# An encoder trunk on one core: when sums of weight blocks are formed by DMA, and in which order ACT and DVE split them

## The chip, the cores and the metric

The kernel runs on one core of a Trainium2 chip. The metric is the device time in microseconds of one execution, the median of several runs. TensorE multiplies matrices (its instructions are PE in the profile, its weight loads PEld), VectorE (DVE) and ScalarE (ACT) work element by element, GpSimd (POOL) and SyncE (SP) here mostly issue DMAs. Each engine works through its own queue in order, and the engines wait for each other through semaphores.

## The reference, cut to what matters

One layer of an encoder on x of 512 tokens by 1024 channels, all in float32:

```
x = x + token_mixer(rmsnorm(x))                      # HGRN2 and mLSTM scans
x = x + cross_attention(rmsnorm(x), rmsnorm(mem))    # 4 heads, 256 memory tokens
x = x + square(relu(rmsnorm(x) @ w_up)) @ w_down     # w_up 1024 x 4096, w_down 4096 x 1024
return rmsnorm(x)
```

The change touches the last product of the cross-attention (`@ w_o`), the weights streamed ahead of it, and above all the third line, the MLP.

## The kernel before

**Float32 out of three products.** Every matrix is split into a high half that TensorE's fp32r takes exactly and a low half that is the rest: ACT writes `hi = copy(src)`, DVE writes `lo = src - hi` (`split_out`, both at L348). A product is hi*hi + hi*lo + lo*hi, three matmuls (L351 to L353, in the MLP L1603 to L1605 and L1314 to L1316). So each weight block costs ACT one copy of 128x1024 and DVE one subtraction of 128x1024 (`wh` and `wl` in the profile) before TensorE can use it. Three buffers each hold the loaded blocks (`st`), the high halves (`wh`) and the low halves (`wl`).

**Seven products in place of eight.** The last product of the cross-attention and the two of the MLP use a scheme of Strassen's kind: a two by two block product in seven block products P1 to P7. Some multiply plain weight blocks (P1, P2, P3), the others sums of weight blocks (P5, P7, P6, P4), and the activation side too enters in sums ("forms"). P7 and P4 build on one chain of sums, P6 on it as well.

**Stages.** The MLP goes through the hidden width in four quarters. Each quarter has an "up" stage (even number `st`: 0, 2, 4, 6; function `up`) and a "down" stage (odd: 1, 3, 5, 7; function `by_blocks`). A stage has 14 jobs: P1 to P7, each for two halves g = 0 and 1 (a and b). A job of an up stage is 24 matmuls of 256 columns, one of a down stage 12 matmuls of 512 columns. The order of the jobs is written out by hand in `MORDER` (L1221): stage 0 has 1a 1b 2a 2b 5a 5b 6a 6b 7a 7b 4a 3a 4b 3b, stages 2, 4 and 6 have 1a 5a 1b 6a 2a 3a 7a 5b 6b 4a 2b 7b 3b 4b, stages 1, 3 and 5 have P1 P5 P6 P2 P7 P3 P4 with a before b, and stage 7 has P1 P5 P2 P6 P3 P7 P4. TensorE's order is this order; on the other engines a scheduler orders the instructions, by their place in the program, a priority (`tc.high_priority`) and added dependencies. `behind(a, b)` adds a dependency without a semaphore: it fixes the order where both stand on one engine. `after(a, b)` adds one with a semaphore.

**Where the sums of weights come from.** Three ways:

- *Form steps.* `make_forms` (L309) forms the sums of the up stages (P5, P7, P6, P4), of stage 1 (P5, P7, P6) and of stages 3, 5 and 7 (P7) in DRAM (`form_P`): a plain load or a copy of another form, issued on SP, then an accumulating DMA issued on POOL. 88 steps in all. They are doled out by a budget: `weights` (L283) is called once for each streamed weight block ahead of the cross-attention's last product, and calls `allow(n)` (L250), which issues steps until the budget is used up; a step on SP costs 1 and one on POOL costs 2. A step on SP is put behind the last weight load, one on POOL waits for the last split on DVE. What is left over is issued in the MLP by `mahead` (L1283), 2 units in every second job.
- *Sums of the down stages.* P5, P6 and P4 of stages 3, 5 and 7 (and P6 and P4 of stage 1) are formed in SBUF, in `msum` (tile `as`): `sum_base` (L1243) loads the first term on SP, `sum_add` (L1253) adds the second on POOL. They are due at a job number: `msplit(n)` (L1257), which splits the weights of job n, first issues what is due by n. P4's sum follows P6's in the same buffer.
- *Loads.* All other blocks are loaded into `st` by `mload`. `mahead(n)` calls `msplit` for jobs n to n+2 and `mload` for n+3 to n+6.

**The activation side.** For stage 0, `norm_half` (L1462) makes the forms of the normalized input; the seventh form P7 is split at L1491, P4 and P3 after it. In an up stage the products leave PSUM through ACT and DVE, and small functions form and split the inputs of the down stage: `first` (difference for P5, L1564), `by_p5` (square for P2, L1568), `second` (P6, L1574), `by_p3` (P3, L1578), `by_p7` (P7, L1582), each for a half g. Those that are not needed at once are called from inside the down stage: `turn` (L1656) lists before which job of the down stage each is put.

Of the kernel before, what the change touches and what calls it, by code (L numbers as in the profile page):

```python
# [80 lines left out]
def trunk(ctx: ExitStack, tc: tile.TileContext, x, mem, wpk, vec, cst, lmask, rmask, rows, out):  # L81
# [60 lines left out]
    def behind(a, b):  # L142

        tc.add_manual_dep(a.ins, b.ins.name, mybir.DependencyInfo(mybir.DependencyClass.NoSync, mybir.DependencyReason.DATA),
                          reason="order of an engine")
# [73 lines left out]
    turn = [0]  # L219
# [30 lines left out]
    def allow(n):  # L250

        budget[0] += n
        while budget[0] > 0:
            o = next(form_steps, None)
            if o is None:
                return
            budget[0] -= 1 if o.ins.engine == mybir.EngineType.SP else 2
            if o.ins.engine == mybir.EngineType.SP:
                behind(o, last_load[0])
            else:  # L260
                after(o, last_made[0])
                accs.append(o)
# [20 lines left out]
    def weights(key):  # L283
        i = SIDX[key]
        with (tc.high_priority() if i > 2 else ExitStack()):
            for n in range(i, i + 3):
                split(n)
            load(i + 3)
        allow(0 if i < 6 else 1 if key[1] == "kv" else 2.5 if i < 45 else 2)
        return hl_tiles[i]  # L290

    mforms = {}
# [959 lines left out]

    def sum_add(st, p, g):  # L1253
        o = mfill(gp, msum[p != "P5"][:, g * 1024:g * 1024 + 1024], st, g, (1, 0) if p == "P4" else (0, 0), True)
        behind(o, last_made[0])

    def msplit(n):  # L1257
        if n >= len(MJ):
            return
        if n not in mhl:  # L1260
            for w in [w for w in due if w[0] <= n]:
                due.remove(w)
                w[1](*w[2:])
            st, p, g = MJ[n]
            mload(n)
            hi, lo = T("wh", 1024, 3, F32R), T("wl", 1024, 3, F32R)
            made = split_out(hi, lo, mst[n])
            last_made[0] = made[1]
            if st % 2 and (p, g) == ("P5", 0):
                for a, b in zip(made, early["P5", 1]):  # L1270
                    behind(a, b)
            if n == 1:
                q_made[0] = made
            mhl[n] = (hi, lo)
            if st % 2 and p == "P6":
                due.append((n + 1, sum_add, st, "P4", g))
            if st % 2 and p in ("P5", "P4") and st < 7:
                q = {"P5": "P5", "P4": "P6"}[p]
                due.append((n + 3, sum_base, st + 2, q, g))
                due.append((n + 7, sum_add, st + 2, q, g))  # L1280
        return mhl[n]

    def mahead(n):  # L1283
        with tc.high_priority():
            for m in range(n, n + 3):
                msplit(m)
            for m in range(n + 3, n + 7):
                mload(m)
        if n % 2:
            allow(2)  # L1290
        return mhl[n]

# [169 lines left out]
    def norm_half(u):  # L1462

        ps = smb()
        for t in range(2):
            pe.transpose(ps[:, t * P:t * P + P], rt[u][:, t:t + 1].to_broadcast([P, P]), ident)
        with tc.high_priority():
            row = sc.activation(rrow[:, u * 256:u * 256 + 256], ps[:, 0:256], AF.Copy)
            if u == 1:
                behind(row, x_made[0][0])  # L1470
            for p, x in ((("P1", fx[0, 0]), ("P2", fx[0, 1])) if u == 0 else (("P5", sraw[0]),)):
                for h in range(2):
                    t_ = times_r(x, u, h)
                    if (p, h) in (("P2", 0), ("P5", 0)):
                        behind(t_, x_made[0][1])
                    made = part_split(p, x, h)
                    if p != "P5" and h == 1:
                        x_made[0] = made
                    if (p, h) == ("P1", 1):
                        for a, b in zip(q_made[0], made):  # L1480
                            behind(a, b)
        if u == 0:
            return
        d = sraw[0]
        x1, x3_, x2_, x4 = fx[0, 0], fx[0, 1], fx[1, 0], fx[1, 1]
        v.tensor_tensor(out=d, in0=d, in1=x1, op=ALU.subtract)
        split_out(*xf["P6"], d)
        for h in range(2):
            times_r(x4, 1, h)
        v.scalar_tensor_tensor(out=x1, in0=d, scalar=-1.0, in1=x4, op0=ALU.mult, op1=ALU.subtract)  # L1490
        p7 = split_out(*xf["P7"], x1)  # L1491
        p4 = split_out(*xf["P4"], x4)
        x3_made = v.tensor_tensor(out=x3_, in0=x3_, in1=d, op=ALU.add)
        for a in (x3_made, p4[1]):
            behind(a, p7[1])
        split_out(*xf["P3"], x3_)
# [53 lines left out]
    def up(st):  # L1550
# [2 lines left out]
        fl = dict(skip_group_check=True)  # L1553

        def square(t, src):
            sc.activation(t, src, AF.Relu)
            sc.activation(t, t, AF.Square)

        def form(p, g, src, buf):
            t = buf(F32R)  # L1560
# [1 line left out]
            forms[p, g] = t  # L1562

        def first(g):  # L1564
            v.tensor_tensor(out=y[3, g], in0=y[2, g], in1=y[3, g], op=ALU.subtract)
            form("P5", g, y[3, g], A4)

        def by_p5(g):  # L1568
            z = y[1, g]
            v.tensor_tensor(out=z, in0=C[g], in1=z, op=ALU.subtract)  # L1570
            square(z, z)
            form("P2", g, z, G4)

        def second(g):  # L1574
# [12 lines left out]
        for n, (p, g) in enumerate(MORDER[st]):  # L1587
            hi, lo = mahead(len(JOBS) * st + n)
            if p == "P1":
                A[g] = smb()  # L1590
            if p == "P2":
                B[g] = mmb()
            if p == "P5":
                C[g] = mmb()
            ps = B[g] if p == "P2" else C[g] if p in ("P5", "P3") else A[g]
            xh, xl = xf[p]
            for k in range(2):
                o = ps[:, k * 256:k * 256 + 256]
                for kt in range(4):
                    z = slice(k * 512 + kt * P, k * 512 + kt * P + P)  # L1600
                    m = slice(kt * 256, kt * 256 + 256)
                    new = k == kt == 0 and p in ("P1", "P2", "P5")
                    pe.matmul(o, lhsT=hi[:, z], rhs=xh[:, m], start=new, stop=False, **fl)  # L1603
                    pe.matmul(o, lhsT=hi[:, z], rhs=xl[:, m], start=False, stop=False, **fl)  # L1604
                    pe.matmul(o, lhsT=lo[:, z], rhs=xh[:, m], start=False, stop=kt == 3, **fl)  # L1605
                after_product()
            if p == "P1":
                y[0, g] = msum[g][:, 2048:2560]
                with tc.high_priority():
                    sc.activation(y[0, g], ps, AF.Copy)  # L1610
            elif p == "P2":
                with tc.high_priority():
                    v.tensor_tensor(out=y[0, g], in0=y[0, g], in1=ps, op=ALU.add)
                square(y[0, g], y[0, g])
                form("P1", g, y[0, g], yt)
            elif p == "P5":
                y[3, g] = T2()[:, 0:512]
                with tc.high_priority():
                    sc.activation(y[3, g], ps, AF.Copy)
            elif p == "P6":  # L1620
                y[1, g] = rrow[:, (1 - g) * 512:(1 - g) * 512 + 512]
                with tc.high_priority():
                    sc.activation(y[1, g], ps, AF.Copy)
            if p in ("P3", "P6") and {("P3", g), ("P6", g)} <= set(MORDER[st][:n + 1]) and (st == 0 or g == 0):
                by_p5(g)
            if p == "P7":
                with tc.high_priority():
                    v.tensor_tensor(out=y[3, g], in0=y[3, g], in1=ps, op=ALU.subtract)
                square(y[3, g], y[3, g])
                form("P4", g, y[3, g], A4)  # L1630
            elif p == "P4":
                y[2, g] = T2()[:, 0:512]
                with tc.high_priority():
                    square(y[2, g], ps)
                    first(g)
                if g == 0:
                    second(g)
                    by_p7(g)
                elif st:
                    by_p5(g)  # L1640
        sta = [{} for _ in range(4)]
# [11 lines left out]
                        fn(h)  # L1653
                    hand(h)

        turn = ((("P1", 1), second, 1), (("P5", 1), by_p3, 0), (("P6", 0), by_p7, 1), (("P2", 0), by_p3, 1))  # L1656
        if st == 6:
            turn = ((("P1", 1), second, 1), (("P5", 1), by_p3, 0), (("P2", 0), by_p3, 1), (("P6", 0), by_p7, 1))
        hand(0)
        hand(1)  # L1660
        return sta, ready
# [97 lines left out]
```

## Time and profile before

| | us |
|---|---|
| median of 3 runs | 827.46 |
| lowest and highest of them | 826.39, 829.32 |
| the profiled execution, its time | 825.79 |
| the profiled execution, its span | 824.0 |
| PE busy in it | 803.1 |
| DVE, ACT, POOL busy | 618.6, 486.1, 95.4 |

The span runs from the first to the last instruction; the rest of the profiled execution's time lies around it. TensorE's clock was granted in full (0.998 of the span). In the views, a line such as L348 can be that of a helper, so that groups are told apart by their tiles: `wl<-st,wh` is the low half of a streamed weight block, `yT<-a` the high half of an activation form. Matmuls overlap, so that one lasts longer than the distance to the next. `SPq` rows are DMA issues, and a DMA's landing is the end of its transfer.

The stages in this execution: the cross-attention's last product ends and stage 0 begins at about 493 us, stage 1 at 539, stage 2 at 579, stage 3 at 619, stage 4 at 657, stage 5 at 697.5, stage 6 at 736.4, stage 7 at 776.7; the last matmul ends at 815.4.

### The profile page before, as it was taken

The page shows a single profiled execution, that of the slowest core. Times are in us where ns is not written, and L with a number is a line of the kernel's source. Part 1 is how long each engine was busy: PE and PEld are TensorE (multiplying, and loading weights), DVE is VectorE, ACT ScalarE, POOL GpSimd, SP SyncE. Part 2 cuts the span into 40 slices and gives each one's busy share as a digit, 9 for nine tenths or more (in the row PEclk, how much of TensorE's full clock was granted, in tenths as well). Part 3 has the DMA queues.
Part 4 walks back from the last instruction along what each step waited for, and adds up shares of the span by engine and source line. Part 5 has one row for each costly group of instructions (what it writes and reads, how often), then busy time and mean ns, then how long its engine had stood idle before and what let it go on. Part 6 is the DMA issues. An engine that isn't in the chain of part 4 may idle for free.

```text
span 824.0 us, 14080 instructions
## 1 busy us (share of the span) xinstructions
PE 803.1 (97%) x5438; PEld 693.2 (84%) x5438; DVE 618.6 (75%) x1033; ACT 486.1 (59%) x854; POOL 95.4 (12%) x130
## 2 busy tenths in 40 slices
PE   8999999999999999999999999899999999999995
PEld 6788788886888989887888889887998899789984
DVE  6568975699469988555567979897489658875995
ACT  5247464445578475455545678773586458546854
POOL 2000111220230011221111003010001000100001
PEclk9999999999999999999999999999999999999999
DMA  7368889588688676887884357768866696668552
GB/s 278 118 238 257 216 181 280 174 197 254 159 230 252 198 221 203 237 193 218 203 224 108 85 122 212 248 163 247 267 199 158 218 282 198 180 200 266 179 153 103
DMA packets 56597, 167.26 MB, mean 203 GB/s; under 512 B 5393, under 2 KB 5521, under 8 KB 56530
## 3 DMA queue, kind: packets, MB, share of 16 engines
q1 hardware_dynamic: 41200, 126.04, 43.7%
q0 software_dynamic: 15040, 39.85, 26.8%
q8 instruction: 43, 0.70, 0.3%
q10 hardware_dynamic: 290, 0.47, 0.2%
q14 instruction: 24, 0.20, 0.1%
HBM read 164.24 MB, written 48.23 MB: 258 GB/s over the span
## 4 chain that ended last, share of the span: by engine, by line
PE 72%; DVE 11%; DMA 6%; issue 5%; ACT 5%; POOL 1%; POOLq 0%; ACTq 0%; DVEq 0%
PE mm L351 11%; PE mm L352 11%; PE mm L353 11%; PE sm L1315 5%; PE sm L1316 4%; PE sm L1314 4%; DVE wl L348 4%; PE sm L1604 2%; DMA st<-in_wpk 2%; PE sm L1605 2%; PE sm L1603 2%; ACT wh L348 2%; DMA st<-form_P 2%; PE mm L1604 1%; PE mm L1605 1%
## 5 line engine op out<-in xcount | busy, mean ns | idle before, releaser
L348 DVE TENSOR_TENSOR wl<-st,wh 128x1024 fp32r<-128x1024 f32 x165 | 201.5, 1224 | 104.0 <-ACT wh L348 103.1
L348 ACT ACTIVATE wh<-st 128x1024 fp32r<-128x1024 f32 x165 | 174.2, 1058 | 171.2 <-PE mm L352 44.0
L351 PE MATMUL mm<-xT,wh 128*128 128x512 f32 x288 | 115.5, 402 | 0.0
L353 PE MATMUL mm<-xT,wl 128*128 128x512 f32 x288 | 113.1, 393 | 0.1
L352 PE MATMUL mm<-xT,wh 128*128 128x512 f32 x288 | 112.8, 392 | 0.3 <-DVE xT L1066 0.3
L305 POOL DMA_DIRECT2D form_P<-in_wpk x44 | 44.7, 1059 | 289.1 <-DVE wl L348 243.5
L1315 PE MATMUL sm<-wl,a 128*128 128x512 f32 x180 | 70.4, 391 | 1.8 <-DVE wl L348 1.8
L1314 PE MATMUL sm<-wh,a 128*128 128x512 f32 x180 | 70.3, 391 | 0.1
L1316 PE MATMUL sm<-wh,a 128*128 128x512 f32 x180 | 70.1, 390 | 0.0
L353 PEld LDWEIGHTS mm<-xT,wl 128*128 128x128 f32 x288 | 54.1, 188 | 11.8 <-DVE wl L348 0.3
L352 PEld LDWEIGHTS mm<-xT,wh 128*128 128x128 f32 x288 | 54.2, 188 | 10.9 <-DVE xT L1066 0.9
L351 PEld LDWEIGHTS mm<-xT,wh 128*128 128x128 f32 x288 | 54.1, 188 | 10.9 <-ACT wh L348 0.3
L305 POOL DMA_DIRECT2D as<-in_wpk x20 | 17.6, 915 | 262.0 <-DVE wl L348 159.8
L1315 PEld LDWEIGHTS sm<-wl,a 128*128 128x128 f32 x180 | 33.8, 188 | 10.0 <-DVE wl L348 3.0
L1314 PEld LDWEIGHTS sm<-wh,a 128*128 128x128 f32 x180 | 33.8, 188 | 7.6 <-ACT wh L348 0.5
L1316 PEld LDWEIGHTS sm<-wh,a 128*128 128x128 f32 x180 | 33.8, 188 | 6.9
L1603 PE MATMUL sm<-yT,wh 128*128 128x256 f32 x128 | 36.3, 284 | 1.7 <-ACT yT L348 1.7
L1604 PE MATMUL sm<-yT,wh 128*128 128x256 f32 x128 | 36.3, 284 | 0.9 <-DVE yT L348 0.9
L1604 PE MATMUL sm<-xT,wh 128*128 128x256 f32 x128 | 36.4, 284 | 0.3 <-DVE xT L348 0.2
L1604 PE MATMUL mm<-xT,wh 128*128 128x256 f32 x128 | 36.3, 284 | 0.2 <-DVE xT L348 0.2
L1603 PE MATMUL sm<-xT,wh 128*128 128x256 f32 x128 | 36.4, 284 | 0.0
L1603 PE MATMUL mm<-xT,wh 128*128 128x256 f32 x128 | 36.3, 284 | 0.0
(388 smaller groups left out, 2114.6 us busy)
## 6 DMA issues: line engine op xcount, KB each, us to landing
st<-in_wpk SPq DMA_DIRECT2D x123, 512.0 KB, 4.4
form_P<-in_wpk POOLq DMA_DIRECT2D x44, 512.0 KB, 9.0
st<-form_P SPq DMA_DIRECT2D x42, 512.0 KB, 5.8
form_P<-in_wpk SPq DMA_DIRECT2D x26, 512.0 KB, 8.0
as<-in_wpk POOLq DMA_DIRECT2D x24, 512.0 KB, 8.4
form_P<-form_P SPq DMA_DIRECT2D x18, 512.0 KB, 10.2
gate<-in_wpk POOLq DMA_DIRECT2D x8, 512.0 KB, 5.8
as<-form_P SPq DMA_DIRECT2D x8, 512.0 KB, 6.6
```

What stands on the lines that cost most here:

```text
L305: return eng.dma_start(out=dst, in_=mblock(st, g, *b), max_dma_last_dim=4096, **kw)
L348: return sc.activation(dst_hi, src, AF.Copy), v.tensor_tensor(out=dst_lo, in0=src, in1=dst_hi.bitcast(F32), op=ALU.subtract)
L351: pe.matmul(ps, lhsT=ah, rhs=bh, start=first, stop=False)
L352: pe.matmul(ps, lhsT=ah, rhs=bl, start=False, stop=False)
L353: pe.matmul(ps, lhsT=al, rhs=bh, start=False, stop=last)
L1314: pe.matmul(ps, lhsT=ah, rhs=bh, start=new, stop=False, **fl)
L1315: pe.matmul(ps, lhsT=ah, rhs=bl, start=False, stop=False, **fl)
L1316: pe.matmul(ps, lhsT=al, rhs=bh, start=False, stop=end and k == 1, **fl)
L1603: pe.matmul(o, lhsT=hi[:, z], rhs=xh[:, m], start=new, stop=False, **fl)
L1604: pe.matmul(o, lhsT=hi[:, z], rhs=xl[:, m], start=False, stop=False, **fl)
L1605: pe.matmul(o, lhsT=lo[:, z], rhs=xh[:, m], start=False, stop=kt == 3, **fl)
```

## The change

- The budget for form steps grows from 1 to 1.25 for each weight of the memory's key and value projections and from 2 to 2.5 for those after them; `mahead` gives no budget during stage 0.
- In stage 0, the split of the weights of job 9 (7b) is put behind the split of the activation form P7 on ACT and on DVE.
- In `msplit`, the base of the next quarter's P5 sum is due 12 jobs after the split of this quarter's P5 (before: 3), the base of the next P6 sum 7 jobs after that of P4 (before: 3), and each add 4 jobs after its base. These adds now wait for DVE's last split with a semaphore (`after`); P4's adds do not.
- In the up stages, `by_p7` of half a is no longer called before the down stage but at its job P5b; `by_p3` of half a moves from P5b to P6a, `by_p7` of half b from P6a to P6b, `by_p3` of half b from P2a to P2b. For stage 7 only `by_p7` of half a is new, at P2b.
- From stage 2 on, for half b, the second form's subtraction is put behind the fifth form's difference on DVE, and its squares behind the fifth form's high half on ACT.

```diff
@@ weights
-        allow(0 if i < 6 else 1 if key[1] == "kv" else 2.5 if i < 45 else 2)
+        allow(0 if i < 6 else 1.25 if key[1] == "kv" else 2.5)
@@ sum_add
-        behind(o, last_made[0])
+        (behind if p == "P4" else after)(o, last_made[0])
@@ msplit
-            if st % 2 and (p, g) == ("P5", 0):
-                for a, b in zip(made, early["P5", 1]):
+            if st % 2 and (p, g) == ("P5", 0) or n == 9:
+                for a, b in zip(made, early["P7" if n == 9 else ("P5", 1)]):
                     behind(a, b)
...
-                due.append((n + 3, sum_base, st + 2, q, g))
-                due.append((n + 7, sum_add, st + 2, q, g))
+                m = n + (12 if p == "P5" else 7)
+                due.append((m, sum_base, st + 2, q, g))
+                due.append((m + 4, sum_add, st + 2, q, g))
@@ mahead
-        if n % 2:
+        if n % 2 and n >= len(JOBS):
             allow(2)
@@ norm_half
-        p7 = split_out(*xf["P7"], x1)
+        p7 = early["P7"] = split_out(*xf["P7"], x1)
@@ up
         def square(t, src):
-            sc.activation(t, src, AF.Relu)
+            o = sc.activation(t, src, AF.Relu)
             sc.activation(t, t, AF.Square)
+            return o
...
         def first(g):
-            v.tensor_tensor(out=y[3, g], in0=y[2, g], in1=y[3, g], op=ALU.subtract)
+            early["diff"] = v.tensor_tensor(out=y[3, g], in0=y[2, g], in1=y[3, g], op=ALU.subtract)
             form("P5", g, y[3, g], A4)
 
         def by_p5(g):
             z = y[1, g]
-            v.tensor_tensor(out=z, in0=C[g], in1=z, op=ALU.subtract)
-            square(z, z)
+            taken = v.tensor_tensor(out=z, in0=C[g], in1=z, op=ALU.subtract)
+            squared = square(z, z)
+            if st and g:
+                behind(taken, early["diff"])
+                behind(squared, early["P5", 1][0])
             form("P2", g, z, G4)
...
                 if g == 0:
                     second(g)
-                    by_p7(g)
                 elif st:
                     by_p5(g)
...
-        turn = ((("P1", 1), second, 1), (("P5", 1), by_p3, 0), (("P6", 0), by_p7, 1), (("P2", 0), by_p3, 1))
+        turn = ((("P1", 1), second, 1), (("P5", 1), by_p7, 0), (("P6", 0), by_p3, 0), (("P6", 1), by_p7, 1), (("P2", 1), by_p3, 1))
         if st == 6:
-            turn = ((("P1", 1), second, 1), (("P5", 1), by_p3, 0), (("P2", 0), by_p3, 1), (("P6", 0), by_p7, 1))
+            turn = ((("P1", 1), second, 1), (("P5", 1), by_p3, 0), (("P2", 0), by_p3, 1), (("P2", 1), by_p7, 0), (("P6", 0), by_p7, 1))
```

## The prediction

> **What bounds the kernel now.** I read the page first, then busy time by stage (windows cut at the borders of the MLP's stages), then PE's timeline around each gap, then ACT, DVE, POOL and the chain of waits at those gaps.
>
> ```profile
> span 824.0 us, 14080 instructions
> PE 803.1 (97%) x5438; PEld 693.2 (84%) x5438; DVE 618.6 (75%) x1033; ACT 486.1 (59%) x854; POOL 95.4 (12%) x130
> ```
>
> TensorE is busy 803.1 of 824.0 us, so 20.9 us is all that scheduling could ever give back. The change deletes no matmul; it can only close gaps, and only gaps inside the stages it touches. The windows of the first two quarters of the MLP show where these are (columns: stretch, length, then busy time of PE, PEld, DVE, ACT, POOL, granted clock, DMA share):
>
> ```profile
> 493.00:539.00 46.00, 42.82 (x348) 41.77 (x347) 42.13 (x52) 37.33 (x58) 7.12 (x4) 1.00 0.73 217
> 539.00:579.00 40.00, 38.69 (x171) 31.40 (x170) 32.97 (x43) 19.56 (x25) 3.55 (x4) 1.00 0.74 211
> 579.00:619.00 40.00, 40.00 (x336) 40.00 (x335) 27.54 (x31) 28.60 (x40) 1.75 (x2) 1.00 0.75 235
> ```
>
> Stage 0 (the first "up") has PE idle 3.2 us and stage 1 (the first "down") 1.3 us; stage 2 has none. So what can be won sits in few places. PE's timeline there (start, duration, instruction, in brackets the idle time before it and what ended it):
>
> ```profile
> 518.12 0.28 PE L1605 MATMUL sm<-yT,wl 128*128 128x256 f32 x1
> 520.15 0.38 PE L1603 MATMUL sm<-yT,wh 128*128 128x256 f32 x1 [1.75 <-ACT yT L348]
> 521.41 0.38 PE L1604 MATMUL sm<-yT,wh 128*128 128x256 f32 x1 [0.88 <-DVE yT L348]
> ...
> 544.13 0.39 PE L1314 MATMUL sm<-wh,a 128*128 128x512 f32 x1
> 545.19 0.50 PE L1315 MATMUL sm<-wl,a 128*128 128x512 f32 x1 [0.67 <-DVE wl L348]
> ...
> 567.89 0.50 PE L1315 MATMUL sm<-wl,a 128*128 128x512 f32 x1 [0.64 <-DVE wl L348]
> ...
> 703.76 0.50 PE L1315 MATMUL sm<-wl,a 128*128 128x512 f32 x1 [0.44 <-DVE wl L348]
> ```
>
> Matmuls of 256 columns follow each other every 0.12 us here and those of 512 columns every 0.23 us, so the time lost is a little more than the bracket: 1.9 + 1.1 = 3.0 us at 518 (job 7a of stage 0), 0.8 us at 544 (job P5a of stage 1), about 0.8 us at 567 (job P3a of stage 1) and 0.6 us at 703 (P5a of stage 5), each with 0.16 us added to its bracket as at 544. Together 5.2 us. That is the ceiling of the change's gain.
>
> **The change part by part, step by step.**
>
> *Splits at the seventh form (stage 0).* Job 7a multiplies weights by the activation form P7, whose high half ACT makes and whose low half DVE makes (both at L348). Why they were late:
>
> ```profile
> 517.61 1.06 ACT L348 ACTIVATE wh<-st 128x1024 fp32r<-128x1024 f32 x1 [2.56 <-DMA st<-form_P]
> 519.05 1.05 ACT L348 ACTIVATE yT<-a 128x1024 fp32r<-128x1024 f32 x1
> ```
> ```profile
> 514.80 1.22 DVE L1490 SCALAR_TENSOR_TENSOR a<-a,a 128x1024 f32<-128x1024 f32 x1
> 518.71 1.23 DVE L348 TENSOR_TENSOR wl<-st,wh 128x1024 fp32r<-128x1024 f32 x1 [2.69 <-ACT wh L348]
> 520.13 1.23 DVE L348 TENSOR_TENSOR yT<-a,yT 128x1024 fp32r<-128x1024 f32 x1 [0.20 <-ACT yT L348]
> ```
> ```profile
> 510.17 7.36 DMA st<-form_P
> ```
>
> P7's source is ready when L1490 ends, at 514.80 + 1.22 = 516.02. But ACT's queue is in order, and the split of the weights of job 9 (7b) stands ahead; its load took 7.36 us and ACT idled 2.56 us for it. The change puts this split behind P7's on both engines. Then P7's high half runs 516.0 to 517.1 and its low half 517.1 to 518.4. PE would be there at 518.24 and use the low half one matmul later: lost 0.1 us in place of 3.0. Gain **2.9 us**. What does the delayed split cost? The weights of 7b land at 517.5, ACT takes them until 518.7, DVE until 519.9; 7b begins 24 matmuls of 0.12 us after 518.3, at 521.2. That covers it by 1.3 us. Bounds: 0, if the shift only makes the next thing late (second rival), and 3.0.
>
> *Sums ahead of the MLP.* Counted in the code, the form steps number 88: 44 loads or copies on SP at cost 1 and 44 adds on POOL at cost 2, 132 units. Before, the streamed weights allow 31 x 2.5 + 16 x 1 + 16 x 2 = 125.5; the last three adds are issued in stage 0. After, 31 x 2.5 + 16 x 1.25 + 16 x 2.5 = 137.5: all are issued by the third weight from the end of the cross-attention's query projection, and the steps before them come one to five weights earlier. The rows are the first and the last of the three, and below them two adds of the next item:
>
> ```profile
> 501.85 1.09 POOL L305 DMA_DIRECT2D form_P<-in_wpk  x1
> ```
> ```profile
> 513.31 1.03 POOL L305 DMA_DIRECT2D form_P<-in_wpk  x1 [5.30 <-DVE wl L348]
> ```
> ```profile
> 554.62 0.88 POOL L305 DMA_DIRECT2D as<-in_wpk  x1 [2.24 <-DMA as<-in_wpk]
> 564.72 0.88 POOL L305 DMA_DIRECT2D as<-in_wpk  x1 [9.23 <-DMA as<-in_wpk]
> ```
> ```profile
> q1 hardware_dynamic: 41200, 126.04, 43.7%
> q0 software_dynamic: 15040, 39.85, 26.8%
> ```
>
> What one costs on the 16 engines follows from the queue rows: 126.04 MB are 240 transfers of 0.524 MB, 43.7% of 824 us is 360 us, so 1.5 us for a load; 39.85 MB are 76 adds in 221 us, so 2.9 us for an add. Taking three adds out of stage 0 frees 8.7 us of the transfer engines just where the load of 7.36 us stood; it secures the first term and I give it no gain of its own. [...]
>
> Where the steps go, the cover is this (same columns as the first windows):
>
> ```profile
> 330.00:385.00 55.00, 55.00 (x261) 44.84 (x260) 31.02 (x58) 27.47 (x64) 9.67 (x11) 1.00 0.89 234
> 385.00:445.00 60.00, 59.74 (x307) 50.25 (x307) 36.07 (x75) 30.25 (x63) 8.92 (x10) 1.00 0.71 182
> ```
>
> At a DMA share of 0.89 PE was busy 55.00 of 55.00 us; the window that takes the last three adds has 0.71. On SP the moved steps stand behind loads that run three weights ahead; on POOL next to the sums of the output projection that follows, which are used one stage later. I take **0**; there is nothing to gain, since PE lacks 0.26 us there in all; upward, one weight late by an add, 2.9 us.
>
> *Seventh form's split of half a moved behind P5b, and the second form's squares behind the fifth's split.* P5a's weights in stages 1, 3, 5 and 7 may only be split after activation form P5b. In stage 1:
>
> ```profile
> 539.59 0.69 DVE L1583 TENSOR_TENSOR as<-as,t 128x512 f32<-128x512 f32 x1
> ...
> 542.11 0.68 DVE L348 TENSOR_TENSOR a<-as,a 128x512 fp32r<-128x512 f32 x1
> ...
> 543.91 1.22 DVE L348 TENSOR_TENSOR wl<-st,wh 128x1024 fp32r<-128x1024 f32 x1
> ```
>
> The two first are by_p7(0), steps of 0.6 us each with their overlap; they leave the queue ahead of the third, which PE waits for: 1.2 us earlier, more than the 0.6 us lost at 703 (the same pattern in stage 5). There the squares, put behind, help as well. Gain there **0.6 us** (0 to 0.6). They come back at job P5b (half b's at P6b), four or five jobs ahead of their use. In stage 1 PE itself comes 2.9 us earlier; the DVE queue comes 1.6 us earlier (low half at 517.1, not 518.7) plus 1.2 us: 2.8. So of the 0.8 us there I count **0.1 us** (0 to 0.8).
>
> *Next quarter's sums begun later.* In stages 1, 3 and 5 the two base loads and two adds of P5's next sums leave the down stage for the next up stage; P6's move four jobs on there. The adds now also wait for DVE; queued behind them on POOL are only more such adds, and those who wait for them are the splits of the next down stage. At 567 it was a load that came late:
>
> ```profile
> 556.67 8.75 DMA st<-in_wpk
> ```
> ```profile
> st<-in_wpk SPq DMA_DIRECT2D x123, 512.0 KB, 4.4
> ```
>
> With the adds at 554.62 and 564.72 and the bases gone, it should be near the median of 4.4 us, 4 us sooner than 8.75: gain **0.8 us** (0 to 0.8). The price falls on the up stage, which streams 14 weights: 14 + 2 loads and 2 adds before, 16 x 1.5 + 2 x 2.9 = 29.8 us of engine time in 40; after, 18 x 1.5 + 4 x 2.9 = 38.6 us. Here are the low halves of jobs 8 and 12 in stage 2, and the first matmul of each job:
>
> ```profile
> 599.59 1.22 DVE L348 TENSOR_TENSOR wl<-st,wh 128x1024 fp32r<-128x1024 f32 x1 [0.71 <-ACT wh L348]
> ```
> ```profile
> 608.64 1.22 DVE L348 TENSOR_TENSOR wl<-st,wh 128x1024 fp32r<-128x1024 f32 x1 [0.79 <-ACT wh L348]
> ```
> ```profile
> 601.71 0.28 PE L1603 MATMUL sm<-yT,wh 128*128 128x256 f32 x1
> ```
> ```profile
> 613.23 0.28 PE L1603 MATMUL mm<-yT,wh 128*128 128x256 f32 x1
> ```
>
> Job 8 is ready 0.9 us early, behind two adds and two bases; job 12, where the two new adds would lie, 3.4 us early. An add beside each load costs the load up to 2.9 us, so job 12 keeps its time by half a microsecond. I charge **0.2 us** for each of three stages, 0.6 us (0 as in stage 2 now, up to the price of the first rival).
>
> Sum: 2.9 + 0.1 + 0.6 + 0.8 - 0.6 = **3.8 us**. The profiled execution took 825.79 us (1.8 us around its span), and would take 822.0. It lies 1.7 us below the median of the three runs shown; off the median, 827.46, the same sum gives **823.7 us**.
>
> **The rivals.**
>
> *Up stages run out of transfers (slower).* 38.6 of 40 us leaves nothing for bunching. The loads of jobs 12 and 13 come late in stages 2, 4 and 6 by 2.9 us for each of the two adds, 5.8 in all against 3.4 us of cover: 2.4 us of wait, and the same lateness then sits in DVE's queue into the next stage. Three times 2.4 is 7.2, against the 4.4 us of gains: 2.8 us slower, **830.3 us**. It decides once a stage loses over 1.5 us. For it: the share; against it: half an add's time for each load, if both queues share evenly, stays within the cover. [...]
>
> *The gain is given back on DVE (no change).* DVE is busy 42.13 of 46 us in stage 0. If it does not use the 2.69 us hole before 518.71, PE comes 2.9 us sooner to P5a's weights but these only 1.2 us sooner: 1.2 + 0.8 + 0.6 - 0.6 = 2.0 us gained, **825.5 us**. Against it: P7's halves are ready to fill the hole.
>
> *The denser form steps cost what they free (no change).* One streamed weight late by one add, 2.9 us: 3.8 - 2.9 = 0.9 gained, **826.6 us**. Against it: PE full at a share of 0.89.
>
> **How the numbers follow.** About 0.3% (2.5 us) is what a measurement of this kernel can tell from no change. Forecast 0.60; up stages 0.13; DVE 0.20; form steps 0.07. Faster 0.60, same 0.27, slower 0.13. The range goes down to all bounds met, 5.2 us off 827.46 with a microsecond for the spread of medians, 821.2, and up past the two no-change cases to a part of the first rival, 829.0; it leaves out that rival's worst. Faster alone would be 821.2 to 825.0.
>
> **What would show it.** Right: no gap at 7a beyond 0.2 us; no add into form_P after 493 us; no P5 base or add inside the down stages; P3a of stage 1 and P5a of stage 5 without a gap; PE full in stages 2, 4 and 6, DMA share there up from 0.75 towards 0.95. Wrong: PE waiting for a weight's low half at jobs 9 to 13 of an up stage, a gap of over 1.5 us at P5a of stage 1, or new gaps before 493 us.

## The result and the profile after

| | before | after |
|---|---|---|
| median of 6 runs each, us | 827.86 | 837.37 |
| lowest and highest | 826.39, 829.41 | 836.32, 838.56 |
| the profiled execution, its time | 825.79 | 836.85 |
| the profiled execution, its span | 824.0 | 835.1 |

The ratio is 1.0113, with a 95% interval of 1.0097 to 1.0128. The change makes the kernel 9.5 us slower; 823.7 was forecast, and the range ended at 829.0.

The first lines of the profile's page after the change:

```profile
span 835.1 us, 14074 instructions
PE 807.6 (97%) x5438; PEld 695.7 (83%) x5438; DVE 617.3 (74%) x1033; ACT 486.1 (58%) x854; POOL 95.2 (11%) x130
```

The instructions of PE are the same 5438, and DVE, ACT and POOL do the same work within 1.3 us. The span grew by 11.1 us while PE's busy time grew by 4.5, so PE both waits more and, somewhere, works more slowly. The windows cut at the new borders show where (stages 0, 1, 2, 4 and 6; columns as in the prediction):

```profile
493.00:536.50 43.50, 42.49 (x347) 41.58 (x346) 41.68 (x52) 37.73 (x58) 4.00 (x1) 1.00 0.58 193
536.50:574.60 38.10, 38.10 (x170) 31.54 (x169) 32.62 (x43) 20.32 (x24) 1.76 (x2) 1.00 0.59 169
574.60:619.50 44.90, 41.12 (x338) 40.53 (x337) 26.41 (x30) 28.04 (x39) 3.45 (x4) 1.00 0.83 245
658.10:702.90 44.80, 42.52 (x338) 41.98 (x337) 26.34 (x30) 28.15 (x39) 3.46 (x4) 0.96 0.83 247
741.50:786.60 45.10, 41.04 (x337) 40.42 (x337) 26.34 (x30) 28.02 (x39) 3.45 (x4) 1.00 0.83 246
```

Stages 0 and 1 became shorter, and stage 1 has no gap left: 38.10 of 38.10 us busy. But the three later up stages take about 45 us in place of 40, with PE idle 2.3 to 4.1 us in each. The DMA share there rose from 0.75 to 0.83 only, not to the 0.95 the prediction looked for. That alone doesn't say that the transfer engines had room: 0.83 of 44.9 us is 37.3 us of transfers, close to the 38.6 us of the prediction's sum, and in a stage of 40 us it would be a share of 0.93. The fourth experiment decides this. Measured from the first matmul of one stage to the first of the next, in us (the last row is the first experiment, told below):

| stage | 0 | 1 | 2 | 3 | 4 | 5 | 6 | 7 |
|---|---|---|---|---|---|---|---|---|
| before | 45.49 | 40.02 | 40.31 | 38.16 | 40.31 | 38.85 | 40.31 | 38.75 |
| after | 43.23 | 38.11 | 44.84 | 38.65 | 44.79 | 38.66 | 45.10 | 39.79 |
| due times put back | 43.23 | 38.11 | 40.31 | 38.11 | 40.31 | 38.11 | 40.31 | 39.10 |

Gained: 2.26 + 1.91 + 0.19 = 4.4 us (stages 0, 1, 5). Lost: 4.53 + 4.48 + 4.79 = 13.8 us in the three up stages, and 0.49 + 1.04 in stages 3 and 7. Together 11.0 us, the growth of the span but for 0.1.

PE's waits from stage 2 on, grouped by who was waited for (total us, times, longest):

```profile
PE mm L1608 <- ACT wh L348: 4.9, 3, 1.8
PE sm L1608 <- DVE t L1633: 2.9, 2, 1.5
PE mm L1610 <- DVE wl L348: 2.3, 3, 0.8
PE sm L1316 <- DVE wl L348: 0.7, 3, 0.3
```

Three times a high half and three times a low half of one weight block: once in each up stage. PE's timeline in stage 2 gives the place:

```profile
609.04 0.28 PE L1610 MATMUL sm<-yT,wl 128*128 128x256 f32 x1
610.88 0.38 PE L1608 MATMUL mm<-yT,wh 128*128 128x256 f32 x1 [1.55 <-ACT wh L348]
...
612.13 0.39 PE L1610 MATMUL mm<-yT,wl 128*128 128x256 f32 x1 [0.76 <-DVE wl L348]
...
616.50 0.36 PE L1608 MATMUL sm<-xT,wh 128*128 128x256 f32 x1 [1.47 <-DVE t L1633]
```

This is job 12 (3b): 1.7 us lost at its high half, 0.9 at its low half, then 1.6 at the first matmul of job 13. Backwards from it, on ACT, in the chain of waits, and on POOL:

```profile
609.76 1.06 ACT L348 ACTIVATE wh<-st 128x1024 fp32r<-128x1024 f32 x1 [6.08 <-DMA st<-in_wpk]
```
```profile
600.26 9.40 DMA st<-in_wpk
```
```profile
597.47 0.86 POOL L305 DMA_DIRECT2D as<-in_wpk  x1 [13.54 <-DVE wl L348]
600.53 0.86 POOL L305 DMA_DIRECT2D as<-in_wpk  x1 [2.20 <-DVE wl L348]
```

ACT idled 6.08 us for a load of 9.40 us, issued between the two adds of P6's next sums. The same load before, where no add was near, and the two adds (from the views of the tiles `st` and `as`, of before and of after):

```profile
DMA to landing us min/median/max: 3.6/3.6/3.6
```
```profile
DMA to landing us min/median/max: 8.3/8.6/9.0
```

9.40 is close to 3.64 + 2 x 2.9, as if the load paid for both adds in full. It landed at 609.66, the second add at 600.53 + 9.00 = 609.53. That sum is a size and not a rule: with one add beside them, two loads of the fourth experiment took 7.6 and 8.2 us.

The wait at job 13 is the echo of the first. On DVE:

```profile
610.85 1.23 DVE L348 TENSOR_TENSOR wl<-st,wh 128x1024 fp32r<-128x1024 f32 x1 [6.39 <-ACT wh L348]
...
615.67 0.68 DVE L1633 TENSOR_TENSOR t<-t,sm 128x512 f32<-128x512 f32 x1
```

The late low half holds up DVE's queue by 6.39 us, and the step at L1633, which job 13 needs, stands behind it and five more, one after the other without a pause. In stage 4 this second wait is missing, yet the stage is as long. There the clock fell (windows of after: first stage 4, then the same place in stage 2; the third column from the end is the granted clock):

```profile
692.00:695.00 3.00, 1.31 (x9) 0.90 (x8) 0.69 (x1) 1.75 (x3) 0.00 (x0) 1.00 0.73 294
695.00:699.00 4.00, 3.42 (x17) 3.42 (x17) 3.96 (x6) 3.94 (x7) 0.00 (x0) 0.60 0.49 141
609.00:612.00 3.00, 0.82 (x5) 0.41 (x3) 1.15 (x1) 2.20 (x4) 0.00 (x0) 1.00 0.55 225
612.00:616.00 4.00, 2.90 (x22) 2.70 (x22) 3.96 (x7) 3.94 (x6) 0.00 (x0) 1.00 0.49 151
```

After a wait of the same length, stage 4 ran for 4 us at a mean granted clock of 0.60 (0.50 in each us from 696 to 699): 17 matmuls start there, 22 in stage 2 in the same time though PE idled in it. The slower matmuls cost about 1.6 us as an estimate, 0.40 of these 4 us, hide the wait at job 13, and count as busy: this is part of the growth of PE's busy time. The waits were 1.52 and 0.76 us in stage 4 and 1.55 and 0.76 us in stage 2, with two matmuls between them each time, and only the first pair was followed by the drop. Why only that one, no run here shows.

### The profile page after: what moved, and what is told of

It is laid out like the page before. It is cut to its first block, busy times and chain, and to the rows that moved or that the text cites. A ratio compares the mean times of both kernels' runs of the same rounds, so it can differ in the third digit from the quotient of the medians.

```text
span 835.1 us, 14074 instructions
## 1 busy us (share of the span) xinstructions
PE 807.6 (97%) x5438; PEld 695.7 (83%) x5438; DVE 617.3 (74%) x1033; ACT 486.1 (58%) x854; POOL 95.2 (11%) x130
## 4 chain that ended last, share of the span: by engine, by line
PE 66%; DVE 14%; DMA 9%; ACT 5%; issue 4%; POOL 1%; POOLq 0%; ACTq 0%; SPq 0%; DVEq 0%
PE mm L351 11%; PE mm L353 11%; PE mm L352 11%; DVE wl L348 5%; PE sm L1316 4%; PE sm L1317 4%; PE sm L1315 4%; DMA st<-form_P 4%; DMA st<-in_wpk 4%; ACT wh L348 2%; PE mm L1316 1%; PE mm L1317 1%; PE mm L1315 1%; DVE a L348 1%; PE mm L1609 1%
```

## The experiments

The theory after these views: each up stage loses its time because both adds of P6's next sums stand in front of one load with little slack (job 12). Its rivals: the count of transfers in the up stage is too high as such; the moved forms or the wait on DVE are at fault. Single runs without an interval are called so.

**1. Due times put back, all else as in the change**

```diff
-                m = n + (12 if p == "P5" else 7)
-                due.append((m, sum_base, st + 2, q, g))
-                due.append((m + 4, sum_add, st + 2, q, g))
+                due.append((n + 3, sum_base, st + 2, q, g))
+                due.append((n + 7, sum_add, st + 2, q, g))
```

> The whole change, but the next quarter's bases and adds are due when they were before (3 and 7 jobs after their P5 or P4). Theory of the adds (the two late adds of P6 in each up stage keep the load of job 12 from landing): the gaps of stages 2, 4 and 6 go, these stages return to 40.3 us each, what the change gains in stages 0 and 1 stays in part (P3a of stage 1 keeps its 0.8 us gap), and the time is 823 to 825 us, 3 to 5 us under the kernel before. Theory of the order (the moved splits and squares made DVE's queue late in the up stages): stages 2, 4 and 6 stay at 43 us or more, 834 to 838 us.

Measured: 821.31 us, ratio to before 0.9927 (0.9913 to 0.9942). This beats both kernels, and is the lowest median of all versions. It is also lower than the 823 to 825 us expected, in part because P3a of stage 1 lost its gap too. Stage 1 and stage 2 in its windows:

```profile
536.20:574.30 38.10, 38.10 (x171) 31.53 (x170) 32.62 (x43) 20.30 (x24) 3.49 (x4) 1.00 0.78 221
574.30:614.60 40.30, 40.30 (x338) 40.30 (x337) 27.83 (x31) 28.17 (x39) 1.73 (x2) 1.00 0.75 233
```

PE is full in both. So the later due times cost some 16 us, and the rivals' 834 to 838 is out. And stage 1's gain does not need them: four adds lie in that stage again (POOL x4), and P3a has no gap.

**2. The later due times and their wait alone, on the kernel before**

```diff
-        behind(o, last_made[0])
+        (behind if p == "P4" else after)(o, last_made[0])
...
-                due.append((n + 3, sum_base, st + 2, q, g))
-                due.append((n + 7, sum_add, st + 2, q, g))
+                m = n + (12 if p == "P5" else 7)
+                due.append((m, sum_base, st + 2, q, g))
+                due.append((m + 4, sum_add, st + 2, q, g))
```

> The kernel before, with the later due times and the adds' wait for DVE and nothing else. Theory of the adds: stages 2, 4 and 6 take 44.5 to 45.5 us each in place of 40.3, the gap at P3a of stage 1 goes, 839 to 842 us. Theory of the order: nothing is lost, 826 to 828 us.

Measured: 842.08 us (one run), beside 827.74 for before: 14.3 us slower. The up stages take 45.70, 45.21 and 45.25 us. These two edits together make the whole loss; the moved forms have no part in it. The first experiment keeps the wait and loses nothing, so it takes the late due times. Whether they would cost as much without the wait was not run. It matters: in the kernel after, the low half that DVE finishes at 600.24 is followed at 600.26 by job 12's load and at 600.53 by the second add, which waited for it, so the wait itself puts the two side by side.

**3. P6's adds as plain copies on the same queue, in the same places**

```diff
-        o = mfill(gp, ..., st, g, (1, 0) if p == "P4" else (0, 0), True)
+        o = mfill(gp, ..., st, g, (1, 0) if p == "P4" else (0, 0), p != "P6")
```

> The whole change, but P6's adds of stages 3, 5 and 7 are plain copies on the same POOL queue at the same times (so P6's and P4's weights there lack their first term); the order of every engine is the same. Theory that it is the accumulating transfer that holds the engines (2.9 us each, both in front of the load): with 1.5 us each the load of job 12 lands after 6 to 7 us in place of 9.4, the gap at job 12 shrinks from 2.6 us to under 0.5 us and stages 2, 4 and 6 take 40.5 to 41.5 us; 825 to 828 us. Theory that any transfer on POOL's queue overtakes the loads: the load still takes 8 us or more and the gap stays over 1.5 us; 832 to 836 us.

This kernel leaves out the first term of P6's and P4's sums in stages 3, 5 and 7. Measured: 825.74 us (one run). The up stages take 40.57, 40.94 and 41.25 us. The load of job 12 and the two copies (views of `st` and `as`):

```profile
DMA to landing us min/median/max: 4.7/4.7/4.7
```
```profile
DMA to landing us min/median/max: 5.1/5.4/5.7
```

The same number of transfers with the same bytes costs the load 1.1 us in place of 5.8. So it isn't the count of transfers or their bytes, it is what an accumulating one takes. The queues' rows show how much, each over 1 us in which POOL's queue was nearly alone (601 to 602 us; after, then with copies; columns: packets, MB, share of 16 engines):

```profile
q0 software_dynamic: 41, 0.17, 97.8%
```
```profile
q0 software_dynamic: 81, 0.33, 80.5%
q1 hardware_dynamic: 37, 0.09, 22.7%
```

The adds move 0.17 MB in that us and fill the engines; the copies move twice that and leave room, and the loads' queue (q1) moves 0.09 MB beside them.

**4. P6's two adds three jobs further apart**

```diff
-                due.append((m + 4, sum_add, st + 2, q, g))
+                due.append((m + (4 if p == "P5" else 3 + 3 * g), sum_add, st + 2, q, g))
```

> The whole change, with the two P6 adds three jobs apart (due 3 and 6 jobs after their bases, so in front of jobs 8 and 12 of the up stage) and everything else the same, all bytes and bases too. Theory of the adds in front of one load: each load meets one add, takes 6 to 7 us, and PE waits under 0.5 us in each of stages 2, 4 and 6; 823 to 826 us. Theory of the sum (38.6 us of transfers in a stage of 40): the bytes are the same, the stages stay at 43 us or more; 833 to 838 us.

Measured: 829.52 us, ratio 1.0039 (1.0024 to 1.0055); 823 to 826 was expected, and that was missed, as were the 833 to 838 of the other theory. The up stages are near what was wanted (41.27, 40.98, 40.31). Stage 6 settles the question of the sum, with the same four adds in it:

```profile
737.00:777.31 40.31, 40.31 (x337) 40.31 (x336) 26.20 (x29) 27.27 (x38) 3.47 (x4) 1.00 0.91 273
```

At a DMA share of 0.91 PE is full; the transfers fit, if they are not bunched. But stages 3 and 7 take 2.7 and 2.1 us more than before (40.87, 40.82). PE at job P5a of stage 3:

```profile
622.89 0.50 PE L1315 MATMUL sm<-wh,a 128*128 128x512 f32 x1 [0.64 <-ACT wh L348]
624.53 0.50 PE L1316 MATMUL sm<-wl,a 128*128 128x512 f32 x1 [1.14 <-DVE wl L348]
```

The second add now lies beside the loads for the first jobs of the down stage, one of which (P1b's) took 8.16 us and kept ACT and DVE from the splits behind it. One add in front of a load was bearable here in the middle of an up stage and not at its end.

**5. P5's sums early again, P6's late; and 6. the reverse**

```diff
-                m = n + (12 if p == "P5" else 7)
+                m = n + (3 if p == "P5" else 7)
```
```diff
-                m = n + (12 if p == "P5" else 7)
+                m = n + (12 if p == "P5" else 3)
```

> The whole change, but only the sums of P6 are due later (7 and 11 jobs after P4); those of P5 are due as before. If the two adds in front of job 12's load are the cause, it still lands after 9 us and stages 2, 4 and 6 take 44 to 45.5 us as in the whole change; 833 to 837 us. If the sum of transfers in the stage is (33 us in place of 38.6 once P5's are out of it), the stages return to 40.3 to 41 us; 822 to 825 us.

> The whole change, but only the sums of P5 are due later (12 and 16 jobs after it); those of P6 as before. Four adds then follow each other in jobs 2 to 4 of an up stage. If loads cannot land beside adds, those of jobs 6 to 9 take 9 us or more and stages 2, 4 and 6 take 42 us or more, 826 to 832 us. If it is only the place in front of job 12 that hurts, the stages stay at 40.3 to 41 us, 821 to 824 us.

Measured: 827.17 and 831.46 us (one run each), beside 827.49 and 826.79 for before. With P6's late neither expectation was met. The up stages take 42.05, 41.92 and 40.83 us: job 12's load still takes 9.33 us, but it was issued at 597.95, which is 22.9 us into its stage and not 25.6 as in the whole change. So PE no longer waits at job 12, and in stage 2 only 1.46 us at job 13 for DVE's L1633. With P5's late, as expected, they take 43.15, 43.35 and 43.38; four adds come close together early in the stage, and PE waits at three jobs (the loads of that stretch, `st`, then PE):

```profile
DMA to landing us min/median/max: 5.7/10.7/11.9
```
```profile
593.02 0.39 PE L1610 MATMUL sm<-yT,wl 128*128 128x256 f32 x1 [0.73 <-DVE wl L348]
596.86 0.39 PE L1610 MATMUL mm<-xT,wl 128*128 128x256 f32 x1 [0.71 <-DVE wl L348]
600.63 0.39 PE L1610 MATMUL sm<-yT,wl 128*128 128x256 f32 x1 [0.63 <-DVE wl L348]
```

Both halves of the edit cost time in the up stages, by the same mechanism at other jobs. It is a matter of bunching, not of P6 alone.

**7. The split of job 9 behind P7's, alone on before**

```diff
-            if st % 2 and (p, g) == ("P5", 0):
-                for a, b in zip(made, early["P5", 1]):
+            if st % 2 and (p, g) == ("P5", 0) or n == 9:
+                for a, b in zip(made, early["P7" if n == 9 else ("P5", 1)]):
...
-        p7 = split_out(*xf["P7"], x1)
+        p7 = early["P7"] = split_out(*xf["P7"], x1)
```

> The kernel before, with the split of job 9's weights behind the seventh form's split and nothing else. By the prediction's first term stage 0 loses 0.1 us in place of 3.0 at job 7a and is 2.3 to 2.9 us shorter, while the load of 7.36 us stays slow, as its adds are still there; the gap at P5a of stage 1 grows by up to 0.5 us; 824.5 to 826 us. If DVE was the limit all along, stage 0 and stage 1 together give less than 1 us: 827 us.

Measured: 828.84 us, ratio 1.0012 (0.9996 to 1.0028): no gain, where 824.5 to 826 us was expected. Stage 0 takes 47.81 us, 2.3 more than before. PE and ACT in it:

```profile
529.74 0.39 PE L1603 MATMUL mm<-yT,wh 128*128 128x256 f32 x1 [2.16 <-ACT yT L348]
531.26 0.39 PE L1604 MATMUL mm<-yT,wh 128*128 128x256 f32 x1 [1.14 <-DVE yT L348]
```
```profile
524.89 1.06 ACT L348 ACTIVATE wh<-st 128x1024 fp32r<-128x1024 f32 x1 [4.60 <-DMA st<-in_wpk]
```

The gap at 7a is gone and a larger one stands at 3a: the next load, beside the third add, took 9.50 us, and ACT's queue waited for that one. Behind it the matmuls start every 0.21 us from 532.13 to at least 534.05, in place of 0.12, as they do in stage 4 of the kernel after at a granted clock of 0.50; that is part of these 2.3 us.

**8. The form steps ahead of the MLP, alone on before**

```diff
-        allow(0 if i < 6 else 1 if key[1] == "kv" else 2.5 if i < 45 else 2)
+        allow(0 if i < 6 else 1.25 if key[1] == "kv" else 2.5)
...
-        if n % 2:
+        if n % 2 and n >= len(JOBS):
             allow(2)
```

> The kernel before, with all form steps ahead of the MLP and nothing else. By the prediction no gap opens before 493 us, and the load in front of job 7a lands 2 us or more earlier without its adds, so that the split of job 9 no longer blocks ACT: the gap at 7a shrinks from 3.0 us to under 1.5 us; 825.5 to 826.5 us. If denser steps cost what they free, gaps of 0.5 us or more stand before 493 us and the time is 827.5 to 830 us.

Measured: 824.62 us, ratio 0.9963 (0.9949 to 0.9978), below what was expected. Stage 0 takes 43.33 us, 2.2 less, with the old order of splits; the load of job 9's weights, whose split stands ahead of P7's, takes 3.24 us in place of 7.36. What is left at 7a is one wait:

```profile
519.23 0.38 PE L1604 MATMUL sm<-yT,wh 128*128 128x256 f32 x1 [0.73 <-DVE yT L348]
```

So the gain of stage 0 comes from moving three adds, not from the order of splits.

**9. The moved forms and squares, alone on before; 10. all but these; 11. all but stage 7's new place**

The ninth has only the diff's edits in `square`, `first`, `by_p5`, the calls ahead of the down stage and `turn`. The tenth is the first experiment without them. The eleventh is the first experiment with, for `st == 6`, `by_p7(g)` called early again and the old `turn`.

> The kernel before, with the seventh form of half a and its followers moved into the down stage and the squares behind the fifth form, nothing else. By the prediction's third term the gaps at P5a of stages 1 and 5 go (0.8 and 0.6 us): 826 to 826.5 us, within what can be told from no change. If the moved splits are late for P7 or P3, new gaps stand at these jobs of the down stages: 828 us or more.

> The version with the whole change but the old due times, without the moved seventh form and squares: so the form steps ahead of the MLP, the split of job 9 behind the seventh form's, and the adds' wait. If the moved forms are what closes the gaps at P5a of stages 1 and 5 (0.8 and 0.4 to 0.6 us), the time is 822.5 to 823.5 us; if the rest closes them, 821 to 821.6 us.

> The version with the whole change but the old due times, and with the old order of the seventh form in the last quarter alone. Stage 7 took 39.10 us there and 38.75 us in the kernel before, with a gap of 0.73 us near its end that was 0.30 us before: if the moved split of half a in stage 7 makes it, stage 7 takes 38.6 to 38.8 us and the time is 820.7 to 821.1 us; if not, 821.3 us.

Measured: 826.66, ratio 0.9987 (0.9971 to 1.0003); 822.71, ratio 0.9946 (0.9928 to 0.9964); 822.40, ratio 0.9941 (0.9919 to 0.9962). In the ninth, stage 1 is 1.9 us shorter, without a gap at P5a or P3a. Stage 0 is 1.5 us longer: behind the old gap at 7a the mean granted clock was 0.57 for 4 us. So PE comes later to stage 1, and this run alone doesn't show that the moved forms close its gaps.

```profile
517.00:521.00 4.00, 1.55 (x11) 1.15 (x10) 2.34 (x2) 3.63 (x5) 0.00 (x0) 1.00 1.07 293
521.00:525.00 4.00, 3.83 (x19) 3.83 (x20) 3.52 (x4) 0.29 (x1) 0.00 (x0) 0.57 0.89 253
```

In the tenth, the gap at P5a of stage 1 is back, which is what the moved forms close; P3a has no gap there without them:

```profile
542.87 0.50 PE L1315 MATMUL sm<-wl,a 128*128 128x512 f32 x1 [0.52 <-DVE wl L348]
```

Its span is 820.2 us against 819.2 for the first experiment, and the two intervals overlap: the moved forms are worth about a microsecond beside the rest, which the times alone don't separate from nothing. The eleventh took 39.82 us for stage 7, not less than the 39.10 of the first, so the new place there is not what makes that stage longer than before.

**12. The first experiment without the wait on DVE**

```diff
-        (behind if p == "P4" else after)(o, last_made[0])
+        behind(o, last_made[0])
```

> The version with the whole change but the old due times, and with its adds not waiting for DVE (as before the change). If the wait is what keeps the adds in the down stages out of each other's way, gaps of 0.4 to 0.9 us come back at P3a of stages 1, 3 or 5 and the time is 822 to 823.5 us against 821.3; if the wait does nothing, 821 to 821.6 us.

Measured: 824.22 us, ratio 0.9967 (0.9952 to 0.9982), above the first experiment's interval and above the time expected. POOL in stage 3, without the wait and then with it, and PE without it:

```profile
627.06 1.76 POOL L305 DMA_DIRECT2D as<-in_wpk  x2 [2.08 <-DVE wl L348]
639.95 0.86 POOL L305 DMA_DIRECT2D as<-in_wpk  x1 [11.13 <-DMA as<-in_wpk]
```
```profile
626.74 0.87 POOL L305 DMA_DIRECT2D as<-in_wpk  x1 [2.07 <-DVE wl L348]
633.81 0.87 POOL L305 DMA_DIRECT2D as<-in_wpk  x1 [6.20 <-DVE wl L348]
636.53 0.87 POOL L305 DMA_DIRECT2D as<-in_wpk  x1 [1.85 <-DVE wl L348]
```
```profile
640.79 0.50 PE L1315 MATMUL sm<-wl,a 128*128 128x512 f32 x1 [0.77 <-DVE wl L348]
```

Without the wait two adds go out at once at 627.06; with it the second of them waits until 633.81. The bunch costs job P7b of stage 3 a late weight, one job ahead of the P3a that was expected: its load, issued at 628.52, took 9.79 us. The wait spaces the adds; it is worth some 2 to 3 us here (0.9967 against 0.9927 in the first experiment and 0.9941 in the eleventh, whose interval overlaps).

## Why the prediction was wrong, point by point

- **The step that failed** is the last term: "An add beside each load costs the load up to 2.9 us, so job 12 keeps its time by half a microsecond. I charge 0.2 us for each of three stages". Both adds stood beside one load, so it came 5.8 us late against 3.4 us of cover. The term measured 4.5 to 4.8 us a stage, 13.8 in all where 0.6 was charged. With P6's sums alone late it was 1.7, 1.6 and 0.5 us (fifth experiment): the rest came only together with P5's, when job 12's load was issued 2.7 us later in its stage. That two adds would meet one load could be read from the page of the kernel before:

```profile
as<-in_wpk POOLq DMA_DIRECT2D x24, 512.0 KB, 8.4
```

  These transfers, 20 of them adds of the MLP, take a median of 8.4 us to land, so two adds that are due one job apart, some 3 us, are in flight together. The prediction had priced just this case as its first rival, at a chance of 0.13, and set it aside by assuming even sharing.
- **The first rival** had place and mechanism right, jobs 12 and 13, and its 2.4 us of wait measured 1.7 + 0.9 = 2.6 at job 12. It was too low in stopping there: it named the lateness that stays in DVE's queue and gave it no price. The follow-up wait of 1.6 us at job 13, or the slowed clock of about 1.6 us in stage 4, made a stage cost twice as much, hence 837.4 and not 830.3. Its headline, transfers running out, was not the limit: in stage 6 of the fourth experiment the same adds are carried with PE full.
- **Even sharing** was the argument against it, and was the author's assumption, not what the runs showed. If the two queues shared the engines evenly, a load's 1.5 us of engine time would grow to 3.0 beside adds, so that it would land about 5.1 us after its issue (3.64 + 1.5), as an estimate from the queue rows and the load of before; it landed after 9.40. The load of 8.75 us at 556.67 in the kernel before doesn't fit even sharing either: two adds, issued at 551.49 and 554.62 and landing after 8.7 and 9.4 us, were in flight beside it, and 8.75 is far nearer to 3.64 + 2 x 2.9 than to 5.1. (Four of the 76 transfers that the prediction counted as adds are plain copies, so that an add is a little dearer than 2.9 us; this changes nothing else.) The queues of the kernel after from 600.5 to 603 us, from there to 610, and in one us of that stretch, 606 to 607:

```profile
q0 software_dynamic: 93, 0.38, 82.8%
```
```profile
q1 hardware_dynamic: 479, 1.32, 53.0%
q0 software_dynamic: 188, 0.64, 47.1%
```
```profile
q0 software_dynamic: 46, 0.19, 94.2%
q1 hardware_dynamic: 17, 0.03, 9.5%
```

  At first only the adds move data (part of this is the about 2 us, as an estimate, that a lone load spends besides its transfer: 3.64 - 1.5). Then the queues share about evenly only in the mean of 7 us. Taken us by us they take long turns: from 606 to 607 the adds have 94.2% of the engines' time and the loads 9.5%. From 603 to 608 the loads' queue moves 0.57 MB, the bytes of hardly more than one load, and it also carried blocks issued later. So even sharing is not what the engines did while the adds were in flight. Why the turns are that long, and why the last part of the one load that mattered landed only at 609.66, these views don't show; that stays open.
- **The split of job 9** was credited 2.9 us. Its gap did go, but alone it gains nothing (seventh experiment): the second rival's bound, "the shift only makes the next thing late", held. The 2.2 us of stage 0 belong to the form steps (eighth), to which the prediction gave "no gain of its own".
- **Sums ahead of the MLP** cost nothing there, as forecast: stage 0 begins at 493 us as before, and the last product of the cross-attention takes 48.00 us against 47.98.
- **The moved forms and squares** closed P5a of stage 1 (the gap is back in the tenth experiment). The 0.8 us at P3a was credited to the later due times, but they are not needed for it: P3a has no gap in the first, ninth, tenth and twelfth experiments, all without them. P5a of stage 5 kept about 0.4 of its 0.6 us in the kernel after, and lost it with the due times put back.
- **The sum of gains** came out as 4.4 us, the 4.4 forecast, from other edits than those credited. The agreement is luck as far as the reasons go: it is that of the ceiling, the gaps that were there.
- **The rivals on DVE and on denser form steps** did not show: the one new wait on DVE in stages 0 and 1 is 0.47 us at job 3a, and there is no gap ahead of 493 us.
- **Open:** why stage 7 takes 0.5 to 1.2 us more with the moved forms (38.64 us without them, 39.10 to 39.82 with them).

## What to carry to other kernels

When a slow transfer is moved, look at which single load it will stand beside, and charge that load at least the transfer's whole time on the engines for each one that can be in flight beside it: 2.9 us for an add here, and beside two adds the load of job 12 took 5.8 us more than the 3.64 it took with none near; beside one add, two loads of the fourth experiment took 4.0 and 4.6 us more than that. A mean share over the stage did not tell of it: PE was full at 0.91 in the fourth experiment and waited at 0.83 in the kernel after. If a wait is removed by reordering a queue, find what made the input late: as long as the cause remains, the wait can move to the next user, as in the seventh experiment, where the 3.0 us at 7a went and waits of 2.16 and 1.14 us came at 3a. Space such transfers on purpose, for instance by letting their issue wait for a step of steady work (821.31 us with that wait in the first experiment, 824.22 without it in the twelfth).

## What the runs showed of the hardware

In the kernel after, accumulating DMAs of 0.524 MB each from POOL moved 0.17 MB from 601 to 602 us with 97.8% of the engines' time; in the third experiment plain copies from the same queue moved 0.33 MB with 80.5%. Beside loads in stage 2 an accumulating DMA took 8.3 to 9.0 us to land, the copy 5.1 to 5.7. Two waits of TensorE close together, 2.3 us in all with two matmuls between them, were followed by 4 us at a mean granted clock of 0.60 in stage 4 of the kernel after and by no such drop in its stage 2: about 1.6 us that no wait shows. The gap at job 7a of stage 0 likewise was followed by 0.57 over 4 us in the ninth experiment and by no drop in the kernel before.
